# A list scheduler's rates: measured TensorE times, a delay for a change of grid, and one port for VectorE and GpSimd

## The chip, the cores and the metric

The kernel runs on one core of a Trainium2 chip. The metric is the device time of the whole program in microseconds (us), the median of several runs. A core has five engines that matter here: TensorE (PE in the profile; its weight loads are PEld), VectorE (DVE), ScalarE (ACT), GpSimd (POOL) and SyncE (SP), which issues the transfers. Each engine executes its own queue strictly in order and waits on semaphores for the others. SBUF is the on-chip memory; PSUM holds the products of TensorE.

## What is computed

The reference is a decoder trunk of two layers for one sequence of 512 tokens and 1024 channels in float32. Each layer has three sub-layers, each with a norm before it and a residual sum behind it:

```python
for l in range(DEPTH):                                   # DEPTH = 2
    h = rms_norm(x, norm_mix[l])
    p_a, p_b, p_c, p_d = jnp.split(h @ w_in[l], splits, axis=-1)
    y = jnp.concatenate([
        rglru_group(p_a, ...),        # a gated linear recurrence
        retention_group(p_b, ...),    # chunked decay attention, 4 heads
        rwkv7_group(p_c, ...),        # RWKV-7, 4 heads
        ssd_group(p_d, ...)],         # Mamba-2 SSD, 4 heads
        axis=-1)
    x = x + y @ w_out[l]
    x = x + memory_cross_attention(rms_norm(x, norm_mem_q[l]), rms_norm(mem, norm_mem_kv[l]), ...)
    x = x + swiglu(rms_norm(x, norm_ffn[l]), ffn_w_in[l], ffn_w_out[l])
return rms_norm(x, norm_final)
```

## The kernel before

**Recording and ordering.** The trunk is written as straight-line code (class `Trunk`), but its calls issue nothing. Each call is recorded as an `Op` with its tiles and its predecessors (`Sched.record`), and `Sched.cost` gives it a duration `dur` and a latency `lat` in nanoseconds, worked out from its shapes. `Sched.order` then makes one static order for all engines. It keeps a clock for each engine. In each step it looks, for each engine, at all operations whose predecessors are placed, and takes the one with the smallest key: the earliest possible start, then the class `cls`, then the largest `rank` (the longest chain of durations behind the operation). `Sched.place` lets an operation start only when a buffer of its tile's kind is free. `Sched.issue` (L511, so that line stands on every row of the profile) emits the operations in that order. The model's times decide the order and nothing else; on the chip each engine runs its part of the order in order.

**Tiles.** The kinds that matter are `s` (a 128x512 float32 tile in SBUF, 70 of them), `u`, `v`, `w` (a block of weights as loaded, its upper part and its lower part, three buffers each), `a` (PSUM banks for the dense products, 3), `b` (PSUM banks for all the rest, 5), `t` (small statistics), `q` (the state in RWKV's loop), `n` (32-row tiles, 2). A name such as `s_1012_1620` is the kind, the number of the recorded operation that first writes it, and a running number.

**Dense products.** A float32 product is made as three float32r products of two-part operands. `weights` loads a block into `u` (SP), casts the upper part `v` (ACT) and subtracts for the lower part `w` (DVE, or POOL for some gate projections, which `project` does late). For 128 output columns `project` issues 24 matmuls 128x512 over one `a` bank: eight blocks of the contraction times (v with the upper part of x, v with its lower part, w with the upper part). The dense products form the chain "d": they keep their recorded order. All other TensorE work (`b` banks, float32, shapes from 128x1 to 128x512) is side work, which the scheduler puts between them.

**The mixers.** `mix` projects w_in and runs the four groups beside each other. `rwkv_pair` (two heads each, so two pairs a layer) first inverts a triangular matrix by a substitution of 62 steps on POOL on tiles `n`, copies the result, sends it out and back in another layout (`fd<-n`, `s<-fd`), and then runs a loop of eight chunks, in which TensorE, DVE and ACT hand one small state (`q`) to each other. `ssd` and `retention` work in four chunks or blocks and end with a norm, `head_norm` and `rsqrt`, in which DVE issues some ten small operations 128x8 one after the other (a Newton iteration). The mixers' results are the input of `w_out`. Then follow `cross` and `ffn`, which are almost wholly dense, and at the end `finish`.

**What orders the work around the change**: `cost` (durations, from which both the model's starts and the ranks come) and `order` (the key, the clocks of the engines).

## Time and profile before

| | |
|---|---|
| median of the runs | 1730.94 us (1729.71 to 1733.04, three runs) |
| span of the profiled execution | 1729.7 us |
| TensorE busy | 1675.9 us, 97% |
| VectorE, ScalarE, GpSimd busy | 1039.6, 632.2, 329.1 us |
| chain of work that ended last | PE 83%, DVE 9%, ACT 2% |

The profile is of one execution. The span counts from its first instruction to its last. TensorE's busy time is modelled at the instructions' ends, so it is read together with the starts of successive matmuls. The granted clock (PEclk) stands as a share of the full 2.4 GHz; 0.50 is the lower level of 1.2 GHz, and a value between is a mean over a stretch that had both.

### The profile page before, as it was taken

To read this page: it belongs to the slowest core of one execution; us is meant where nothing else is said; L and a number is where in the kernel's file an instruction comes from. 1 tells how busy PE (TensorE), PEld (TensorE's weight loads), DVE (VectorE), ACT (ScalarE), POOL (GpSimd) and SP (SyncE) were. 2 spreads that over 40 slices of the span, in tenths; PEclk is the share of its full clock that TensorE was granted. 3 is DMA by queue.
4 is the path that set the end of the run, shared out by engine and by line. 5 is a ranking of instruction groups with operands and counts; after the bars stand their busy time and mean duration, and the time that the engine had idled before them with its cause. 6 is when DMAs were issued, how large, how long until landed. Compare 5 with 4: busy or idle time off the path is not lost.

```text
span 1729.7 us, 21681 instructions
## 1 busy us (share of the span) xinstructions
PE 1675.9 (97%) x8344; PEld 1355.9 (78%) x8344; DVE 1039.6 (60%) x1712; ACT 632.2 (37%) x976; POOL 329.1 (19%) x370
## 2 busy tenths in 40 slices
PE   7999999999999999999989999989999999999997
PEld 6687777888788888888878877767887888888886
DVE  7777669775664555432467767596665655544323
ACT  6434244543542233322344333354444423332221
POOL 3367724300000000000141875241000000000001
PEclk9899999999999999999999999999999999999998
DMA  7433321441333333333453333115322333333331
GB/s 231 129 83 101 87 55 37 152 128 50 98 97 98 95 89 97 95 101 119 137 153 88 88 89 90 37 37 173 95 74 86 98 97 89 94 98 91 93 95 63
DMA packets 296648, 168.99 MB, mean 98 GB/s; under 512 B 19424, under 2 KB 283872, under 8 KB 296416
## 3 DMA queue, kind: packets, MB, share of 16 engines
q1 hardware_dynamic: 296544, 167.60, 33.4%
q8 instruction: 66, 1.08, 0.3%
q14 instruction: 38, 0.31, 0.1%
HBM read 156.04 MB, written 9.44 MB: 96 GB/s over the span
## 4 chain that ended last, share of the span: by engine, by line
PE 83%; DVE 9%; ACT 2%; issue 1%; DMA 1%; POOL 1%; SPq 0%; DVEq 0%; ACTq 0%; POOLq 0%
PE a L511 73%; PE b L511 9%; DVE s L511 5%; DVE t L511 2%; DVE w L511 1%; ACT s L511 1%; ACT v L511 1%; DMA s<-s 1%; DVE q L511 0%; POOL s L511 0%; DMA s<-in_lora_dram 0%; POOL n L511 0%; SPq L511 0%; DMA n<-nd 0%; ACT L511 0%
## 5 line engine op out<-in xcount | busy, mean ns | idle before, releaser
L511 PE MATMUL a<-s,v 128*128 128x512 f32 (+1 forms) x4012 | 1252.7, 391 | 15.9 <-ACT s L511 9.3
L511 PEld LDWEIGHTS a<-s,v 128*128 128x128 f32 x4012 | 748.0, 191 | 177.6 <-DVE s L511 10.9
L511 PE MATMUL a<-s,w 128*128 128x512 f32 (+1 forms) x2006 | 782.8, 390 | 3.8 <-DVE w L511 1.9
L511 ACT CAST v<-u 128x1024 fp32r<-128x1024 f32 (+3 forms) x275 | 282.0, 1026 | 673.2 <-PE a L511 390.2
L511 PEld LDWEIGHTS a<-s,w 128*128 128x128 f32 x2006 | 382.8, 191 | 83.7 <-POOL w L511 2.3
L511 DVE TENSOR_TENSOR w<-u,v 128x1024 fp32r<-128x1024 f32 (+3 forms) x242 | 294.7, 1219 | 148.3 <-ACT v L511 145.3
L511 DVE TENSOR_TENSOR s<-a,s 128x512 f32<-128x512 f32 (+1 forms) x132 | 90.7, 691 | 259.5 <-PE a L511 240.4
L511 POOL TENSOR_TENSOR w<-u,v 128x1024 fp32r<-128x1024 f32 x33 | 81.9, 2483 | 657.3 <-ACT v L511 646.0
L511 ACT ACTIVATE s<-s 128x512 f32<-128x512 f32 (+3 forms) x229 | 142.8, 628 | 128.6 <-DVE s L511 111.9
L511 POOL TENSOR_TENSOR s<-s,s 128x512 f32<-128x512 f32 (+3 forms) x45 | 57.1, 1286 | 589.2 <-ACT s L511 555.9
L511 PEld LDWEIGHTS b<-s,s 128*128 128x128 f32 (+3 forms) x1268 | 127.2, 165 | 43.7 <-issue 15.3
L511 PE MATMUL b<-s,s 128*128 128x128 f32 (+8 forms) x1268 | 154.6, 269 | 5.5 <-DVE s L511 4.0
L511 DVE TENSOR_TENSOR s<-s,s 128x512 f32<-128x512 f32 (+3 forms) x184 | 133.0, 726 | 26.4 <-ACT s L511 18.5
L511 DVE SCALAR_TENSOR_TENSOR s<-s,s 128x512 f32<-128x512 f32 (+2 forms) x164 | 122.8, 752 | 13.3 <-ACT s L511 12.7
L511 DVE TENSOR_TENSOR s<-s,a 128x512 f32<-128x512 f32 (+1 forms) x49 | 33.2, 678 | 102.0 <-PE a L511 102.0
L511 POOL TENSOR_TENSOR s<-n,n 32x31 f32<-32x31 f32 (+15 forms) x124 | 73.4, 592 | 97.4 <-DMA n<-nd 88.0
L511 POOL TENSOR_TENSOR n<-n,s 32x31 f32<-32x31 f32 (+15 forms) x124 | 81.6, 658 | 9.7
L511 ACT COPY s<-b 64x128 f32<-64x128 f32 (+3 forms) x108 | 35.0, 325 | 113.9 <-PE b L511 93.3
L511 PE MATMUL a<-v,s 128*128 128x260 f32 (+1 forms) x256 | 68.3, 344 | 0.0
L511 DVE SCALAR_TENSOR_TENSOR s<-s,prm,s 128x512 fp32r<-128x512 f32 (+3 forms) x78 | 63.0, 832 | 7.4 <-ACT s L511 7.3
L511 PE MATMUL b<-cst,s 128*128 128x128 f32 (+2 forms) x312 | 47.6, 266 | 10.7 <-DVE s L511 8.4
L511 PEld LDWEIGHTS b<-cst,s 128*128 128x128 f32 x312 | 38.6, 159 | 20.5 <-issue 8.0
(93 smaller groups left out, 835.0 us busy)
## 6 DMA issues: line engine op xcount, KB each, us to landing
u<-in_ffn_w_in_dram SPq DMA_DIRECT2D x88, 512.0 KB
u<-in_w_in_dram SPq DMA_DIRECT2D x52, 512.0 KB
u<-in_ffn_w_out_dram SPq DMA_DIRECT2D x32, 512.0 KB
u<-in_mem_wv_dram SPq DMA_DIRECT2D x16, 512.0 KB
u<-in_w_out_dram SPq DMA_DIRECT2D x16, 512.0 KB
u<-in_mem_wq_dram SPq DMA_DIRECT2D x16, 512.0 KB
u<-in_mem_wo_dram SPq DMA_DIRECT2D x16, 512.0 KB
u<-in_mem_wk_dram SPq DMA_DIRECT2D x13, 512.0 KB
```

What stands on the lines that cost most here:

```text
L511: op.fn(*[real(x) for x in op.args], **{k: real(x) for k, x in op.kw.items()})
```

## The change

Comments and docstrings go; they produce nothing. What stays differs in two methods. In `cost`, the durations of TensorE's operations are new: a transpose 85 ns for 112; a float32r product `max(111, 6 + 0.4405 w)`, which makes a 128x512 product 231.5 ns for 217; a float32 product, which used to be proportional to its size, has a floor, 116 ns where the stationary operand has at most 64 columns and 219 ns above it. A scan on DVE costs twice as much, a copy on POOL about half. Each TensorE operation gets a `grid` (64 or 128 rows by 64 or 128 columns). Operations of DVE with two wide operands in SBUF, some single-operand ones from SBUF to SBUF, and all POOL operations get the flag `port`. In `order`, an operation with that flag starts in the model only when the other engine's last flagged operation has ended; among TensorE operations of equal start and class, one with the grid of the last one goes first, ahead of the rank; and a change of grid advances the model's time by 93 ns.

```diff
             if fn == "transpose":
-                op.dur = 112.0
+                op.dur = 85.0
             else:
-                m, w = _free(ins[0]), _free(ins[1])
-                op.dur = (max(2 * m, w) / 2.4 if ins[0].ap.dtype == F32R else max(m, w) * 1.667) + 4
+                k, m, w = ins[0].shape[0], _free(ins[0]), _free(ins[1])
+                op.grid = HD if k <= HD else P, HD if m <= HD else P
+                if ins[0].ap.dtype == F32R:
+                    op.dur = max(111.0, 6 + 0.4405 * w)
+                else:
+                    op.dur = 2 * max(58.0 if m <= HD else 109.5, 2.5 + w / 1.2)
...
+            elif fn == "tensor_tensor_scan":
+                rate = 2.08
...
-            rate = {"tensor_tensor": 2.3, "tensor_copy": 3.5, "memset": 0.83}.get(fn, 1.2)
+            rate = {"tensor_tensor": 2.3, "tensor_copy": 1.9, "memset": 0.83}.get(fn, 1.2)
...
+        if op.eng in ("DVE", "POOL") and not op.bytes:
+            wide = [x for x in ins if isinstance(x, Ref) and x.root.kind not in "ab" and _free(x) > 1]
+            op.port = len(wide) > 1 or op.eng == "POOL" or (
+                fn in ("tensor_scalar", "tensor_copy") and len(wide) == 1 and not in_psum and out.root.kind not in "ab")
...
+                    if op.port:
+                        t = max(t, held[other[e]])
...
-                    key = (t, op.cls if op.cls != 2 or side < 1500.0 else 0, -op.rank, op.n)
+                    key = (t, op.cls if op.cls != 2 or side < 1500.0 else 0, op.grid != grid if e == "PE" else False, -op.rank, op.n)
...
+            if e == "PE" and op.grid != grid:
+                grid = op.grid
+                t += 93.0
...
+            if op.port:
+                held[e] = end
```

No instruction is added, dropped or reshaped, and no tile or buffer count changes. The line that issues moves from L511 to L535. What changes is the order on every engine. Three places in the first layer show it.

The first place is GpSimd in the second pair's substitution (`n_1010`, steps of two operations each; `w<-u,v` is the lower part of a block of weights for a late projection). Before:

```order
L511 TENSOR_TENSOR s_1012_1620<-n_1006_1513,n_1010_1601 32x112
L511 TENSOR_TENSOR n_1010_1601<-n_1010_1601,s_1012_1620 32x4x28
L511 TENSOR_TENSOR w_2128_2076<-u_2126_1807,v_2127_2057 128x1024
L511 TENSOR_TENSOR s_1012_1620<-n_1006_1513,n_1010_1601 32x87
L511 TENSOR_TENSOR n_1010_1601<-n_1010_1601,s_1012_1620 32x3x29
L511 TENSOR_TENSOR s_1012_1620<-n_1006_1513,n_1010_1601 32x60
L511 TENSOR_TENSOR n_1010_1601<-n_1010_1601,s_1012_1620 32x2x30
```

After:

```order
L535 TENSOR_TENSOR w_2291_2331<-u_2289_2071,v_2290_2307 128x1024
L535 TENSOR_TENSOR s_1012_1664<-n_1006_1606,n_1010_1584 32x112
L535 TENSOR_TENSOR n_1010_1584<-n_1010_1584,s_1012_1664 32x4x28
L535 TENSOR_TENSOR s_1748_1574<-s_1748_1574,t_1971_2311 128x512
L535 TENSOR_TENSOR w_2321_2378<-u_2319_2169,v_2320_2367 128x1024
L535 TENSOR_TENSOR s_1012_1664<-n_1006_1606,n_1010_1584 32x87
L535 TENSOR_TENSOR s_2060_2157<-s_2060_2157,s_2061_2119 128x512
L535 TENSOR_TENSOR n_1010_1584<-n_1010_1584,s_1012_1664 32x3x29
L535 TENSOR_TENSOR w_2354_2443<-u_2352_2252,v_2353_2423 128x1024
L535 TENSOR_TENSOR s_1012_1664<-n_1006_1606,n_1010_1584 32x60
```

One `w` and no full-width tile stood between the substitution's last 20 steps; now eight `w` and six full-width tiles do.

The second place is TensorE in the loop of the second pair, where `ssd`'s products (`b_1654`, `b_1672`, `b_1685`) stand beside it; `a` are dense products. Before:

```order
L511 MATMUL b_1210_2566<-s_1110_2217,s_1004_1231 64x64
L511 MATMUL b_1654_2561<-s_1635_1965,s_1648_2017 64x128 x3
L511 MATMUL b_1672_2612<-cst,t_1399_1554 128x128
L511 MATMUL b_1685_2614<-cst,s_1432_1391 128x128
L511 MATMUL b_1672_2612<-cst,t_1399_1554 128x128
L511 MATMUL b_1685_2614<-cst,s_1498_1488 128x128
L511 MATMUL a_2201_2486<-s_118_592,v_2199_2237 128x512
L511 MATMUL b_1672_2612<-cst,t_1399_1554 128x128
```

After:

```order
L535 MATMUL b_1654_2788<-s_1635_2722,s_1648_2764 64x128
L535 MATMUL b_1175_2812<-s_1105_2575,s_1097_1266 128x128
L535 MATMUL a_2391_2569<-v_2431_2600,s_23_197 128x512
L535 MATMUL a_2391_2569<-w_2432_2617,s_23_197 128x512
L535 MATMUL a_2391_2569<-v_2431_2600,s_24_211 128x512
L535 MATMUL b_1672_2836<-cst,t_1399_1713 128x128 x3
L535 MATMUL b_1685_2841<-cst,s_1432_1372 128x128
L535 MATMUL b_1685_2841<-cst,s_1498_1472 128x128
```

Side products of one kind stand together, and so do dense ones.

The third place is TensorE at the end of the mixers: the transposes that close retention's norm (`b_2007`, `b_2012`), ssd's (`b_2249`, `b_2254`) and the second pair's (`b_1264`). Before (`b_1264` has been issued 20 rows earlier, `a_2322` is a projection of w_in):

```order
L511 MATMUL a_2322_2948<-s_117_537,w_2321_2694 128x512
L511 MATMUL b_2007_2877<-cst,s_1749_1690 128x128 x2
L511 MATMUL b_2012_2883<-cst,s_1749_1690 128x128 x2
L511 MATMUL a_2322_2948<-s_120_521,v_2320_2665 128x512
L511 MATMUL b_2249_3006<-cst,t_2239_2964 128x128 x4
L511 MATMUL b_2254_3012<-cst,t_2239_2964 128x128 x4
L511 MATMUL a_2322_2948<-s_121_558,v_2320_2665 128x512
```

After (`a_2469` is the first product of w_out, begun before the last four chunks of the loop):

```order
L535 MATMUL b_1236_3044<-s_1110_2608,s_1004_1229 64x64
L535 MATMUL b_2007_3091<-cst,s_1748_1574 128x128 x2
L535 MATMUL b_2012_3100<-cst,s_1748_1574 128x128 x2
L535 MATMUL b_2249_3153<-cst,t_2239_3093 128x128 x4
L535 MATMUL b_2254_3160<-cst,t_2239_3093 128x128 x2
L535 MATMUL b_1264_3163<-cst,s_945_978 128x128 x4
L535 MATMUL b_2254_3160<-cst,t_2239_3093 128x128 x2
L535 MATMUL a_2469_2888<-s_2453_3175,v_2467_2733 128x512
```

All three norms' transposes now stand together behind the loop's last product, with no dense product between them; before, projections of w_in stood between and behind them.

## Rows read from the trace of the kernel before

**Rows 1.** The page: busy time of each engine, and the chain that ended last.

```profile
PE 1675.9 (97%) x8344; PEld 1355.9 (78%) x8344; DVE 1039.6 (60%) x1712; ACT 632.2 (37%) x976; POOL 329.1 (19%) x370
PE 83%; DVE 9%; ACT 2%; issue 1%; DMA 1%; POOL 1%; SPq 0%; DVEq 0%; ACTq 0%; POOLq 0%
```

**Rows 2.** Windows by stage: start:end, length, busy (instructions) by engine, clock, DMA.

```profile
0.00:100.00 100.00, 84.55 (x452) 70.20 (x453) 77.39 (x158) 50.85 (x84) 28.80 (x24) 0.91 0.55 165
100.00:350.00 250.00, 242.27 (x1417) 191.39 (x1417) 185.44 (x373) 101.04 (x175) 132.85 (x162) 0.99 0.32 88
...
850.00:900.00 50.00, 44.42 (x277) 40.48 (x276) 28.91 (x29) 18.89 (x29) 28.33 (x14) 0.93 0.48 138
900.00:1200.00 300.00, 286.10 (x1614) 222.69 (x1613) 217.41 (x434) 120.26 (x204) 134.15 (x165) 0.98 0.31 85
1200.00:1700.00 500.00, 499.55 (x2216) 406.09 (x2216) 256.57 (x331) 167.38 (x236) 0.00 (x0) 1.00 0.32 92
```

**Rows 3.** Windows of 50 us around the ends of the mixers, same columns.

```profile
250.00:300.00 50.00, 46.67 (x283) 36.64 (x283) 46.71 (x126) 23.71 (x43) 21.95 (x17) 0.97 0.14 43
...
1100.00:1150.00 50.00, 46.89 (x288) 36.43 (x287) 45.07 (x112) 25.31 (x46) 20.21 (x16) 0.97 0.10 33
1150.00:1200.00 50.00, 44.62 (x186) 34.56 (x185) 37.91 (x66) 22.85 (x34) 13.89 (x8) 0.93 0.43 132
```

**Rows 4.** Timeline of PE in pair two's loop: start, us, instruction, count, [idle before].

```profile
231.63 0.50 PE L511 MATMUL a<-s,v 128*128 128x512 f32 x1
231.97 0.40 PE L511 MATMUL a<-s,w 128*128 128x512 f32 x1
232.20 0.38 PE L511 MATMUL b<-s,s 128*128 128x128 f32 x2
...
234.03 0.48 PE L511 MATMUL a<-s,v 128*128 128x512 f32 x1
234.44 0.44 PE L511 MATMUL b<-q,s 64*64 64x64 f32 x4
```

**Rows 5.** Timeline of PE: two chunks' first products of the loop; transposes after a wait.

```profile
244.73 0.38 PE L511 MATMUL b<-q,s 128*128 128x128 f32 x2
...
250.11 0.39 PE L511 MATMUL b<-q,s 128*128 128x128 f32 x2
...
293.69 1.79 PE L511 MATMUL b<-cst,s 128*128 128x128 f32 x15 [2.08 <-DVE s L511]
```

**Rows 6.** DVE from 100 to 350 us by form: count | busy, mean ns | idle before.

```profile
L511 DVE SCALAR_TENSOR_TENSOR t<-t,t 128x8 f32<-128x8 f32 x31 | 6.6, 217 | 0.5
...
L511 DVE TENSOR_REDUCE t<-s 128x8 f32<-128x512 f32 x8 | 5.5, 682 | 2.6 <-ACT s L511 2.4
L511 DVE TENSOR_SCALAR t<-t 128x8 f32<-128x8 f32 x8 | 5.2, 654 | 0.1
...
L511 DVE SCALAR_TENSOR_TENSOR q<-b,t,cst 128x128 f32<-128x128 f32 x14 | 4.9, 348 | 10.0 <-PE b L511 10.0
...
L511 DVE TENSOR_TENSOR t<-t 128x8 f32<-128x8 f32 x15 | 4.6, 310 | 0.2
...
L511 DVE SCALAR_TENSOR_TENSOR s<-s,prm,b 128x512 f32<-128x512 f32 x3 | 2.2, 745 | 1.2 <-PE b L511 1.2
```

**Rows 7.** Timeline of DVE: a small operation of the Newton iteration, twice.

```profile
27.45 2.29 DVE L511 SCALAR_TENSOR_TENSOR t<-t,t 128x4 f32<-128x4 f32 x1
...
297.19 0.17 DVE L511 SCALAR_TENSOR_TENSOR t<-t,t 128x8 f32<-128x8 f32 x1
```

**Rows 8.** Timeline of POOL: weight blocks at 27 us and in pair two's substitution.

```profile
27.35 2.36 POOL L511 TENSOR_TENSOR w<-u,v 128x1024 fp32r<-128x1024 f32 x1 [0.96 <-ACT v L511]
...
202.32 2.37 POOL L511 TENSOR_TENSOR w<-u,v 128x1024 fp32r<-128x1024 f32 x1 [6.49 <-ACT v L511]
```

**Rows 9.** Timeline of SP's issues: the transfers behind pair two's substitution.

```profile
207.18 2.39 SPq L511 DMA_DIRECT2D fd<-n  x2
...
215.21 3.93 SPq L511 DMA_DIRECT2D s<-fd  x8
```

More of the change, by code (lines that the diff above doesn't have):

```diff
@@ L233 @@
     __slots__ = ("n", "eng", "fn", "args", "kw", "dur", "lat", "preds", "succ", "left", "ready", "end", "rank", "cls",
-                 "roots", "first", "chain", "bytes", "start", "table")
+                 "roots", "first", "chain", "bytes", "start", "table", "grid", "port")
 def _free(x):
@@ L364, in cost @@
         op.bytes = 0
-        op.table = None
+        op.table = op.grid = None
+        op.port = False
         op.lat = 170.0
@@ L373, in cost @@
             op.lat = 200.0
+            op.grid = P, P
             if fn == "transpose":
-                op.dur = 112.0
+                op.dur = 85.0
             else:
-                m, w = _free(ins[0]), _free(ins[1])
-                op.dur = (max(2 * m, w) / 2.4 if ins[0].ap.dtype == F32R else max(m, w) * 1.667) + 4
+                k, m, w = ins[0].shape[0], _free(ins[0]), _free(ins[1])
[4 more added lines that the diff above has]
+                    op.dur = 2 * max(58.0 if m <= HD else 109.5, 2.5 + w / 1.2)
         elif op.eng == "ACT":
@@ L426, in order @@
         table = None
+        grid = P, P
+        held = {"DVE": 0.0, "POOL": 0.0}
+        other = {"DVE": "POOL", "POOL": "DVE"}
         INF = float("inf")
```

## The prediction

> **What bounds the kernel now.** The page first: TensorE is busy 1675.9 of 1729.7 us and carries 83% of the chain that ended last, VectorE another 9% [rows 1]. No instruction changes, so the kernel can gain only what TensorE waits, what it loses at a lower clock, and what it pays for the order of its own products. The windows by stage say where that is [rows 2]. In cross attention and FFN TensorE works 499.55 of 500 us at clock 1.00: nothing to gain, and dense products in a fixed order leave the scheduler little to spoil. What is idle lies in the head (0 to 100: 15.5 us, clock 0.91), in the two mixers (100 to 350: 250 - 242.27 = 7.7 us; 900 to 1200: 300 - 286.10 = 13.9 us) and between the layers (850 to 900: 5.6 us, clock 0.93). The windows of 50 us place the mixers' share at their ends and give the clock: 0.97, 0.97 and 0.93 over 46.67, 46.89 and 44.62 busy us cost 0.03 x 46.67 = 1.4, 0.03 x 46.89 = 1.4 and 0.07 x 44.62 = 3.1 us [rows 3]. So both mixers together now lose 7.7 + 1.4 + 13.9 + 4.5 = **27.5 us**. That is the number to beat.
>
> **Part 1: fewer changes between kinds of products.** In the loop, a dense product behind another starts the next one 0.23 us later (231.97 to 232.20); the first one behind side work takes 0.34 (231.63 to 231.97); one with side work of another grid on both sides 0.41 (234.03 to 234.44) [rows 4]. So a return costs 0.11 and a departure to another grid 0.07 to 0.1; I take 0.1 for each. Counted in the two orders, grid changes fall from 317 to 288 (29 fewer) and returns to a dense product behind another grid from 124 to 112 (12 fewer): 41 x 0.1 = 4.1 us. Returns behind side work of the same grid fall from 156 to 121; each costs between 0 (no row shows one bare) and the 0.11 above, so 0 to 3.9 us, of which I take 1.6, nearer the lower end because a change of grid is what the dear rows have in common. Part 1: **-5.7 us** (-4.1 to -8.0). It lies on TensorE, which is the bound, so nothing hides it except a wait for another engine right behind.
>
> **Part 2: the ends of the mixers.** Here the order does something the diff does not say. On GpSimd the second pair's substitution now shares the queue with eight weight blocks and six full-width operations. A block takes 2.37 us [rows 8], and it cannot start before TensorE frees one of three buffers, which happens once a projection: 24 x 0.23 = 5.5 us. So the substitution ends later, and the pair's loop, counted in TensorE work since the start, moves from about 194 to 241 us (second layer: 1029 to 1069), while gate projections and the recurrent group come earlier. Before the last four chunks only six dense products are left, and behind the loop none (third place of the order). Three terms for each layer:
>
> *The tail.* Behind the last chunk DVE has to issue, before w_out can go on, 32 small operations, two reduces, two multiplications with statistics, two operations with a PSUM bank and seven more of full width. With the rows: the reduces 2 x 0.68; the eleven of full width at 0.7, an estimate between the reduce's 0.68 and the 0.745 of an operation with a PSUM bank (7.7), or all at 0.745 (8.2); the small ones at 0.17 where nothing is in the way [rows 7] or at the mean of what they took in this stage, (31 x 0.217 + 15 x 0.310 + 8 x 0.654) / 54 = 0.305 [rows 6]. That is 1.4 + 7.7 + 5.4 = 14.5 or 1.4 + 8.2 + 9.8 = 19.4 us. TensorE's own work meanwhile is 20 transposes at 1.79 / 15 = 0.12 [rows 5] and some thirty small products at the 0.11 of [rows 4], together about 6. It waits 8.5 to 13.4 us; I take 10.6, a little under the middle, since GpSimd has three operations there against the weight blocks of before.
>
> *The loop.* A chunk's chain is nowhere bare. It is at most 5.4 us (244.73 to 250.11, with dense products in it [rows 5]) and at least some 3.2: three DVE steps of some 0.35 [rows 6], an ACT copy that I put at the same, and four visits of TensorE of 0.4 to 0.5 [rows 4, 5]. I take the middle, 4.3. The last four chunks have 3 to 4 us of other TensorE work each, say 3.5: 4 x 0.8 = 3.2 us of waiting (0 to 7.6).
>
> *The clock.* A stretch of this much idle time cost 1.4 to 3.1 us at the lower level behind it [rows 3]; 2.3.
>
> Sum for a layer 10.6 + 3.2 + 2.3 = 16.1, both 32.2. Two waits on the first pair's data, at about 109 and 953 us, stand at the same products in both orders; I leave 2 us for them. So the mixers lose 34.2 after and 27.5 before: **+6.7 us**.
>
> **Part 3: head and change of layer.** In the new order all eight products of the memory's keys come before the first norm's results are used; before, the norm stood in the middle of them. DVE's small operations for that norm still stand behind weight blocks. The products no longer wait for them, the norm's users do, and there is no other work for TensorE behind. Of 15.5 and 5.6 idle us [rows 2] the early part is loading and stays. I take 0 for each, with 3 us to both sides: one block of 2.36 us in or out of DVE's way, with its clock [rows 8].
>
> **Part 4: DVE and GpSimd kept apart.** That the two hinder each other is plain: a small operation that takes 0.17 us took 2.29 while GpSimd's block ran from 27.35 for 2.36 us [rows 7, 8]. But the plan keeps them apart only in its own time, and the queues have no wait for it; it is worth what the new order happens to avoid. Its share is inside the 0.17 and 0.305 of part 2 and the 3 us of part 3. The planner flags every GpSimd operation, pure fills too, so it plans some avoidable delays, none of which is a wait on the chip. The Trainium skill, page "SBUF — State Buffer", section "Who interferes with whom", says that the shared port goes to one engine for a whole instruction and the other fully blocks, and that a DVE instruction with two SBUF inputs contends only with a GpSimd instruction that reads SBUF, not with one that only writes. The rows agree with the first half; no row shows the second. By that rule each of the tail's three GpSimd operations, half as wide as the 2.37 us block and so some 1.2 us each, blocks DVE for up to 3.6 us in a layer, and the tail goes from 14.5 to 18.1; if the port were shared, it would stay at 14.5. Both are inside the range above.
>
> **The sum.** -5.7 + 6.7 + 0 = +1.0 on the profiled span of 1729.7, which gives 1730.7. The median is 1.2 above that span, so the time is **1732 us**.
>
> **Rivals.** *Keeping apart pays (faster).* If the new order really spares DVE its collisions, the small operations run at 0.17 wherever TensorE waits for them. The tails come to 8.5 us each, the loop to 2, the clock to 1.4: 12 a layer, 24 + 2 - 27.5 = -1.5. Head and change of layer give 3 each for the same reason: -1.5 - 6 - 5.7 = -13, which is **1718 us**. For it: the small operations in this stage lost 54 x (0.305 - 0.17) = 7.3 us [rows 6, 7]. Against it: most of that was beside dense work and cost nothing, and the new tail has no dense work.
>
> *GpSimd's queue holds up the second loop (slower).* From the freeing of the last block's buffer to the loop TensorE has some 16.4 us of work in the new order. The chain that must fit is the block, 2.4 us [rows 8], with its cast ahead of it, put at half of that, the last step of 0.3, and the way out and back, from the first issue to the end of the last 215.21 + 3.93 - 207.18 = 12.0 [rows 9], with a landing behind it that no row bounds and that is left at 0 to 2: 16 to 18 us. It decides when that exceeds 16.4. Then the loop starts 0 to 2 us late, its chunks run at the 5.4 of before (7.6 us of waiting instead of 3.2), and the tail stands at its upper end: 2 + 7.6 + 13.4 + 3.1 = 26 a layer at worst, 24.5 in the middle; 49 + 2 - 27.5 - 5.7 = +18, which is **1749 us**. For it: no dense product is left to fill in, so every us of delay is lost. Against it: the late start alone is worth 2 us, and the rest takes the upper value of each term.
>
> *The change does little that it says.* Only part 1 is real and the ends of the mixers lose what they lost: 1725 us. It is the lower edge of my forecast.
>
> **How the numbers follow.** My forecast, 1732, with its own range 1724 to 1740, has 0.42; faster through separation, 1712 to 1726, has 0.29; the late loop, 1738 to 1755, has 0.29. A measurement tells about 0.2%, or 3.5 us, from no change. Of the forecast's 0.42, 0.25 lies within that, 0.08 below and 0.09 above. So faster 0.08 + 0.29 = 0.37, the same 0.25, slower 0.09 + 0.29 = 0.38. The range 1714 to 1750 leaves out about 0.08 below and 0.1 above.
>
> **What would show it.** Right: cross attention and FFN unchanged; 100 to 350 and 900 to 1200 us each lose about 16 us in idle time and clock, now in one block before w_out, released by DVE's small operations; fewer starts of 0.34 between dense products. Rival one: TensorE's wait before w_out is under 9 us and the head under 13 idle. Rival two: GpSimd's blocks in the substitution wait for buffers, TensorE waits before the loop's first product, and its chunks stand 5 us apart. Wrong altogether: waits in places that the order leaves as they were, or another time for cross attention or FFN.

## The result and the profile after

The changed kernel is slower: **1741.3 us** (four runs, 1740.9 to 1742.5) against 1731.6 us for the kernel before beside it, a ratio of **1.006 with an interval of 1.0046 to 1.0074**. The profiled executions differ by the same: spans of 1739.6 and 1729.7 us. Medians, ranges and intervals, here and below, leave out two executions that ran slow, one of the kernel without the port rule (1781.5 us) and one with TensorE's times alone (2056.3 us). The forecast had been 1732 and no change. 1741 lies inside the whole range (1714 to 1750) and on the side to which the prediction gave 0.38, but above the forecast's own 1724 to 1740 and among the times of the late-loop rival, 1738 to 1755.

Where the 9.9 us are is best read at one product that both traces hold. The dense products keep their order, so the start of one and the same matmul can be compared:

| the same dense product, about | before, us | after, us | later by | added in this stage |
|---|---|---|---|---|
| first w_in products behind the head | 101.9 | 100.5 | -1.4 | -1.4 |
| within w_out, first layer | 335.7 | 346.3 | +10.6 | **+12.0** (mixers) |
| end of FFN, first layer | 850.3 | 860.9 | +10.6 | 0.0 |
| first w_in products, second layer | 933.4 | 941.1 | +7.7 | -2.9 (change of layer) |
| behind w_out, second layer | 1220.7 | 1230.1 | +9.4 | **+1.7** (mixers) |
| end of FFN, second layer | 1717.7 | 1725.7 | +8.1 | -1.3 |

The rest, 1.8 us, is in the last 14 us. Nearly all of the loss is made in the two mixers. The page agrees: TensorE is no longer busy for 97% of the span, as in [rows 1].

```profile
PE 1673.1 (96%) x8344; PEld 1358.0 (78%) x8344; DVE 1025.0 (59%) x1712; ACT 634.9 (36%) x976; POOL 317.3 (18%) x370
```

The windows of the changed kernel, cut at those products and at the ends of the mixers, say how. Columns as in [rows 2]: window, length, busy us of PE, PEld, DVE, ACT and POOL, clock, DMA share, GB/s.

```profile
100.50:291.50 191.00, 184.95 (x1081) 146.00 (x1080) 136.34 (x240) 73.44 (x123) 118.74 (x148) 1.00 0.32 85
300.00:333.00 33.00, 22.01 (x162) 17.68 (x162) 25.76 (x89) 11.11 (x25) 6.50 (x8) 0.84 0.09 24
333.00:346.30 13.30, 13.07 (x51) 10.59 (x51) 7.02 (x10) 4.67 (x7) 0.00 (x0) 0.87 0.19 59
941.10:1150.00 208.90, 202.53 (x1175) 160.42 (x1174) 149.72 (x275) 81.61 (x136) 123.33 (x157) 1.00 0.33 88
1150.00:1186.00 36.00, 24.91 (x180) 19.82 (x178) 28.65 (x94) 12.99 (x30) 6.49 (x8) 0.86 0.08 23
1186.00:1200.00 14.00, 13.76 (x54) 11.06 (x54) 7.53 (x11) 4.70 (x7) 0.00 (x0) 0.88 0.18 57
```

And the same cut through the kernel before:

```profile
101.90:285.00 183.10, 178.22 (x1124) 139.11 (x1122) 132.50 (x284) 69.86 (x129) 110.74 (x148) 1.00 0.29 75
285.00:335.70 50.70, 47.85 (x224) 39.15 (x225) 41.78 (x73) 24.00 (x35) 20.45 (x12) 0.97 0.32 99
933.40:1137.00 203.60, 197.47 (x1203) 154.25 (x1202) 143.08 (x299) 74.22 (x136) 111.62 (x150) 1.00 0.29 76
1137.00:1192.90 55.90, 48.52 (x214) 37.20 (x213) 45.22 (x80) 24.36 (x36) 22.54 (x16) 0.91 0.31 91
```

Idle time plus clock, as in the prediction, gives this table (the 0.3 us from 291.5 to 300 go with the first line):

| | before | after |
|---|---|---|
| first layer, up to the last chunks | 4.9 | 6.3 |
| first layer, from there into w_out | 2.85 + 0.03 x 47.85 = 4.3 | 11.2 + 0.16 x 22.0 + 0.13 x 13.07 = 16.4 |
| second layer, up to the last chunks | 6.1 | 6.4 |
| second layer, from there into w_out | 7.4 + 0.09 x 48.52 = 11.8 | 11.3 + 0.14 x 24.9 + 0.12 x 13.76 = 16.5 |
| both mixers | **27.1** | **45.6** |

So by these windows the two ends lose 16.4 and 16.5 us. The clock's share in that is too large: the stretches at the lower level lie largely in the waits, and the mean of a long window charges them to the busy time. Summed over windows of 5 us, the clock costs 3.6 and 3.8 us in the changed mixers, the ends lose 14.9 and 15.1, and both mixers together 42.7 for 27.3 before.

The timeline of TensorE in the changed kernel shows the bare end. Columns: start, us, instruction and count, in brackets the idle time before it and its releaser.

```profile
316.95 0.44 PE L535 MATMUL b<-q,s 64*64 64x64 f32 x4
317.32 1.95 PE L535 MATMUL b<-cst,s 128*128 128x1 f32 x16
319.20 0.65 PE L535 MATMUL b<-s,s 128*64 128x64 f32 x4
319.78 1.12 PE L535 MATMUL b<-cst,s 128*128 128x128 f32 x4
326.61 1.11 PE L535 MATMUL b<-cst,s 128*128 128x128 f32 x4 [5.71 <-POOL s L535]
...
331.26 0.49 PE L535 MATMUL a<-s,v 128*128 128x512 f32 x1 [1.29 <-ACT s L535]
```

Retention's norm is closed by two groups of four transposes, one for each of its result tiles (the third place of the order shows the first group alone). From the first group, at 319.78, to the second, at 326.61, TensorE's queue holds nothing else. The releaser named is GpSimd, but it is only the last link: VectorE's chain of small operations ahead of it runs from 319.3 with one pause of 0.15 us. One piece of it:

```profile
324.99 0.16 DVE L535 SCALAR_TENSOR_TENSOR t<-t,t 128x8 f32<-128x8 f32 x1
...
325.20 1.37 DVE L535 SCALAR_TENSOR_TENSOR t<-t,t 128x8 f32<-128x8 f32 x3
```

```profile
325.51 1.04 POOL L535 TENSOR_TENSOR s<-s,t 128x512 f32<-128x512 f32 x1 [5.73 <-DVE t L535]
328.19 2.67 POOL L535 TENSOR_TENSOR s<-s,s 128x512 f32<-128x512 f32 x2 [1.64 <-ACT s L535]
```

Three small operations at 325.20 take 1.37 us together where 0.17 is the time of one: GpSimd's operation starts at 325.51, and they are done when it is. The Trainium skill, page "SBUF — State Buffer", section "Who interferes with whom", says that the other engine fully blocks; this trace agrees, with one collision of some 1 us at a layer's end, not the three (3.6 us) that the prediction held possible.

The clock falls around the wait. From 320 to 325 us, with TensorE busy for 0.89 us of 5, it is at 0.50. It was not the long wait that took it down: that begins at 320.9, and the window before, with TensorE busy for 4.73 of 5, is already at 0.93. What came ahead is the loop's last chunks, in which TensorE waited for 3.67 us of 17. Every window up to 340 holds some of the lower level:

```profile
300.00:317.00 17.00, 13.33 (x115) 10.61 (x115) 12.60 (x39) 4.11 (x12) 1.74 (x4) 1.00 0.16 44
315.00:320.00 5.00, 4.73 (x41) 4.33 (x39) 3.23 (x11) 1.78 (x5) 1.04 (x1) 0.93 0.02 3
320.00:325.00 5.00, 0.89 (x4) 0.49 (x3) 4.71 (x29) 1.33 (x3) 0.00 (x0) 0.50 0.01 2
325.00:330.00 5.00, 3.36 (x16) 3.11 (x16) 3.97 (x14) 2.05 (x4) 2.86 (x3) 0.55 0.00 2
330.00:335.00 5.00, 3.19 (x8) 2.13 (x9) 4.99 (x8) 2.87 (x6) 0.86 (x1) 0.79 0.00 0
335.00:340.00 5.00, 5.00 (x20) 4.00 (x20) 1.65 (x3) 2.03 (x3) 0.00 (x0) 0.87 0.00 0
```

Why are the ends bare? GpSimd's timeline says it. The copy behind the second pair's substitution starts at 258.49 in the changed kernel; it used to start at 207.22, with the first of [rows 9]. It stands behind the eight blocks of weights, seven of them with a wait of 1.6 to 3 us for ScalarE's cast, which mostly waits for TensorE:

```profile
248.34 2.50 POOL L535 TENSOR_TENSOR w<-u,v 128x1024 fp32r<-128x1024 f32 x1 [2.00 <-ACT v L535]
250.79 0.28 POOL L535 TENSOR_TENSOR s<-n,n 32x60 f32<-32x60 f32 x1
...
254.61 2.40 POOL L535 TENSOR_TENSOR w<-u,v 128x1024 fp32r<-128x1024 f32 x1 [1.58 <-ACT v L535]
...
258.49 2.10 POOL L535 COPY n<-n 32x1024 f32<-32x1024 f32 x1
```

So the loop of the second pair begins at 278.6 us for 227.4 before, and the projections that used to lie beside its last chunks have been used up by then.

### The profile page after: what moved, and what is told of

Read it like the earlier page. It is cut to its first block, busy times and chain, and to the rows that moved or that the text cites. A ratio compares the mean times of both kernels' runs of the same rounds, so it can differ in the third digit from the quotient of the medians.

```text
span 1739.6 us, 21636 instructions
## 1 busy us (share of the span) xinstructions
PE 1673.1 (96%) x8344; PEld 1358.0 (78%) x8344; DVE 1025.0 (59%) x1712; ACT 634.9 (36%) x976; POOL 317.3 (18%) x370
## 5 line engine op out<-in xcount | busy, mean ns | idle before, releaser
L535 PE MATMUL a<-s,v 128*128 128x512 f32 (+1 forms) x4012 | 1240.3, 389 | 18.9 <-ACT s L535 11.4
L535 PEld LDWEIGHTS a<-s,v 128*128 128x128 f32 x4012 | 745.8, 190 | 182.7 <-DVE s L535 13.0
L535 PE MATMUL a<-s,w 128*128 128x512 f32 (+1 forms) x2006 | 778.6, 388 | 0.3 <-DVE w L535 0.3
L535 ACT CAST v<-u 128x1024 fp32r<-128x1024 f32 (+3 forms) x275 | 282.4, 1027 | 717.3 <-PE a L535 438.5
L535 PEld LDWEIGHTS a<-s,w 128*128 128x128 f32 x2006 | 380.6, 190 | 80.8 <-issue 0.7
L535 DVE TENSOR_TENSOR w<-u,v 128x1024 fp32r<-128x1024 f32 (+3 forms) x242 | 290.7, 1202 | 166.1 <-ACT v L535 164.1
L535 DVE TENSOR_TENSOR s<-a,s 128x512 f32<-128x512 f32 (+1 forms) x132 | 90.6, 690 | 264.7 <-PE a L535 246.9
L535 POOL TENSOR_TENSOR w<-u,v 128x1024 fp32r<-128x1024 f32 x33 | 79.1, 2398 | 622.3 <-ACT v L535 621.7
L535 ACT ACTIVATE s<-s 128x512 f32<-128x512 f32 (+3 forms) x229 | 142.7, 628 | 128.2 <-DVE s L535 104.9
L535 POOL TENSOR_TENSOR s<-s,s 128x512 f32<-128x512 f32 (+3 forms) x45 | 50.5, 1138 | 642.8 <-ACT s L535 566.1
L535 PE MATMUL b<-s,s 128*64 128x64 f32 (+8 forms) x1268 | 152.8, 269 | 12.8 <-DVE s L535 8.1
L535 PEld LDWEIGHTS b<-s,s 128*128 128x128 f32 (+3 forms) x1268 | 124.7, 164 | 46.8 <-issue 15.9
L535 DVE TENSOR_TENSOR s<-s,s 128x512 f32<-128x512 f32 (+3 forms) x184 | 131.0, 717 | 18.8 <-ACT s L535 12.2
L535 DVE SCALAR_TENSOR_TENSOR s<-s,s 128x512 f32<-128x512 f32 (+2 forms) x164 | 116.1, 712 | 8.8 <-ACT s L535 7.8
L535 DVE TENSOR_TENSOR s<-s,a 128x512 f32<-128x512 f32 (+1 forms) x49 | 33.2, 677 | 104.4 <-PE a L535 104.4
L535 POOL TENSOR_TENSOR s<-n,n 32x31 f32<-32x31 f32 (+15 forms) x124 | 73.3, 591 | 97.2 <-DMA n<-nd 82.9
L535 POOL TENSOR_TENSOR n<-n,s 32x31 f32<-32x31 f32 (+15 forms) x124 | 82.4, 664 | 8.8
L535 PE MATMUL a<-v,s 128*128 128x260 f32 (+1 forms) x256 | 71.5, 353 | 2.6 <-DVE s L535 2.6
L535 ACT COPY s<-b 64x128 f32<-64x128 f32 (+3 forms) x108 | 34.8, 324 | 89.4 <-PE b L535 70.5
L535 DVE SCALAR_TENSOR_TENSOR s<-s,prm,s 128x512 fp32r<-128x512 f32 (+3 forms) x78 | 57.4, 759 | 11.0 <-ACT s L535 11.0
L535 PE MATMUL b<-cst,s 128*128 128x128 f32 (+2 forms) x312 | 50.4, 277 | 14.1 <-POOL s L535 11.4
L535 PEld LDWEIGHTS b<-cst,s 128*128 128x128 f32 x312 | 40.5, 164 | 22.9 <-POOL s L535 12.2
```

What stands on the lines that cost most here:

```text
L535: op.fn(*[real(x) for x in op.args], **{k: real(x) for k, x in op.kw.items()})
```

## The experiments

Two theories went in. **P**: the port rule in the plan makes the second substitution late and the ends bare. **G**: the grid rule, which bunches side products, does. In what follows every time is a median beside the kernel before on the same chip, with the ratio's interval.

**Without the port rule.**

```diff
-                    if op.port:
-                        t = max(t, held[other[e]])
```

> The changed kernel without the two lines by which a flagged operation waits for the other engine in the plan; TensorE's new times, the grid rule and the two new rates stay. Theory P (the port rule in the plan empties the ends of the mixers: it makes GpSimd's second substitution late, weight blocks slip in, and the dense products are used up before the last chunks): the two bare tails of some 16 us a layer go, since in this order 139 and 119 dense products stand among the last 100 side products of the mixers where the changed kernel has none; the tails lose at most what they lost before, so the time is 1722 to 1730 us. Rival G (the grid rule, which bunches side products, makes the ends bare): it is still in, so the time stays at 1737 to 1742 us.

Measured: 1766.9 us (1755.0 to 1769.9), 1.0182 (1.0127 to 1.0236). Both theories missed. The ends are covered, as P said, but another loss appears in the middle. With nothing held back, side work is drawn forward, VectorE is busy for 9.80 of 10 us, TensorE waits 2.65 us in ten, and then the clock falls:

```profile
215.00:225.00 10.00, 7.35 (x69) 5.08 (x70) 9.80 (x25) 3.03 (x7) 1.35 (x3) 1.00 0.31 80
225.00:270.00 45.00, 44.60 (x175) 34.95 (x175) 19.60 (x56) 6.18 (x16) 5.51 (x4) 0.51 0.05 12
270.00:285.00 15.00, 14.42 (x79) 10.10 (x78) 12.38 (x29) 6.36 (x13) 4.70 (x3) 1.00 0.10 25
```

It stays at its lower level for 45 us in which TensorE is busy for 44.6: 0.49 x 44.6 = 22 us, more than the whole difference in question. TensorE issues side products with a dense one now and then in that stretch. Summed over windows of 5 us, this kernel is idle for 10 us more than the kernel before and loses 27 us more to the clock. What follows: in this order the port rule also does good. That the wait of 2.65 us is what took the clock down is argued, not shown; if it is, a wait can cost many times its own length.

**The port rule alone, in the kernel before.** The same lines and flags are put into the kernel before, with its old TensorE times and without the grid rule.

> The kernel before with the port rule alone (old TensorE times, no grid rule, old rates). Theory P: the same late substitution, with nine weight blocks in it and 15 and 17 dense products among the last 100 side products; bare tails, some 10 us a layer more than before: 1738 to 1752 us. Rival G: as before, 1729 to 1734 us.

Measured: 1779.8 us (1777.0 to 1783.7), 1.0275 (1.0247 to 1.0303). P's direction, but far beyond its price, and the place is in part another one. The ends lose (310 to 360 us: 8.5 idle, clock 0.73), and TensorE also waits in the middle of both mixers, for VectorE, once for 8.1 us in the first and once for 11.7 in the second. The row has the total, the number of waits and the longest:

```profile
PE a L522 <- DVE s L522: 31.6, 15, 11.7
```

That the rule, with TensorE's work underrated in the plan, delays side work so far that dense products wait for it is an explanation that no run isolates.

**The grid rule alone** (with the two new rates of VectorE and GpSimd; no port rule, old TensorE times).

```diff
-                op.dur = 85.0
+                op.dur = 112.0
...
-                    if op.port:
-                        t = max(t, held[other[e]])
```

> The changed kernel without the port rule and with the old TensorE times: what is left is the grid rule with its 93 ns and the two rates. 296 changes of grid for 317 before and 539 alternations of dense and side products for 585, dense products at the ends as in the kernel before (130 and 105 among the last 100). Theory P: 3 to 6 us under the kernel before, 1725 to 1729 us. Rival G: bare ends, 1738 to 1742 us.

Measured: 1734.7 us (ten runs, 1729.2 to 1741.5), 1.0022 (1.0002 to 1.0042). G falls for the grid rule by itself: the ends are not bare. P's gain of 3 to 6 us does not come either. From 205 to 285 us TensorE is idle for 8.1 us (1.1 in the kernel before), more than the 3 to 6 us that fewer changes of grid were to give.

```profile
205.00:285.00 80.00, 71.87 (x446) 55.91 (x447) 65.88 (x169) 31.58 (x59) 21.86 (x17) 0.96 0.13 37
```

**Without the preference for the last grid.**

```diff
-                    key = (t, op.cls if op.cls != 2 or side < 1500.0 else 0, op.grid != grid if e == "PE" else False, -op.rank, op.n)
+                    key = (t, op.cls if op.cls != 2 or side < 1500.0 else 0, -op.rank, op.n)
```

> The changed kernel without the preference for the last grid in the key; port rule, 93 ns and times stay. Four weight blocks in the second substitution for eight, 100 dense products among the last 100 side products in both layers, and 312 grid changes. If bare ends are what costs, whichever rule makes them: the tails go, some 12 us in all, and part 1's gain goes with them: 1728 to 1735 us. If the port rule costs by something other than the bare ends (DVE delayed by the plan all over): 1738 to 1745 us.

Measured: 1735.4 us (1733.2 to 1739.1), 1.0020 (1.0009 to 1.0031); 6 us under the changed kernel, 0.4 above what bare ends as the cause allow. The ends still lose, 7.8 and 7.9 us idle with clocks of 0.85 and 0.89 (300 to 345 and 1150 to 1195 us): with four weight blocks in the substitution for eight, the pair's loop starts at 246 us for 279. So beside the port rule the grid rule has a share after all: its preference doubles the blocks.

**Late weights on VectorE, in the changed kernel.** Theory **T** from here on: the bare ends are what the change costs, and they come from the late substitution. Rivals: **V**, VectorE's load makes the ends long; **C**, the clock decides, wherever a wait takes it down.

```diff
-        late = lambda c0: self.project(w, c0, hat, self.G)
+        late = lambda c0: self.project(w, c0, hat)
```

> The changed kernel with one word gone: the late gate projections take the lower parts of their weights on VectorE instead of GpSimd (33 blocks). No weight block stands in GpSimd's second substitution any more (eight before), 83 dense products stand among the last 100 side products of the mixers in both layers (none in the changed kernel), 36 among the last 40. Theory T (the bare tails, which come from the late substitution, are what the change costs): each layer's loss from the last chunks to w_out falls from some 16 us to 5 to 8; VectorE's 33 x 1.2 = 40 us more are beside dense work; 1720 to 1731 us. Rival V (VectorE is what the tails wait for, so more work on it keeps them long): 1738 to 1750 us. Rival C (a wait that takes the clock to its lower level decides, wherever it lies): a stretch of 20 us or more at 0.50, 1750 us or more.

Measured: 1728.6 us (1725.8 to 1735.0), 0.9987 (0.9974 to 1.0000): 12.7 under the changed kernel, as T said; V falls. The trace puts it where T has it: of 13.0 us in the span, 12.8 are in the mixers, and 11.1 of these are idle time at the ends, 11.2 and 11.3 us before the edit and 5.7 each after it. But the copy behind the substitution still starts at 225.3, and with the clock the ends lose more than the 5 to 8 us a layer that T allowed. (The edit moves 14 blocks, not the 33 of the expectation: VectorE's go from 216 to 230. The other 19 are the values' weights, four a layer, and those of the head and the change of layer.)

**The same in the kernel before, as a control.**

> The same word gone in the kernel before, as a control: 85 and 107 dense products among the last 100 side products for 75 and 97, so the ends stay covered. Theory T: nothing to cure, 1727 to 1735 us, so what the edit gives the changed kernel comes from its tails. Rival V: VectorE's added 40 us lengthen the ends here too, 1738 us or more.

Measured: 1710.1 us (1709.5 to 1712.7), 0.9878 (0.9863 to 0.9893). The control gains more than the case, 21 us where no end was bare, so the time of the first is no proof by itself; what speaks for T there is the place. TensorE is idle for 10.5 us less and loses 10 us less to the clock. What changed beside the order is that GpSimd's blocks of 2.5 us meet fewer of VectorE's small operations. Counted in the trace of the kernel before, 97 of the 142 operations 128x8 ran beside no GpSimd operation at all, and none of these took over 0.173 us; the seven that ran beside a weight block took 1.9 us on average. In this kernel two do. Two of their forms, over the whole run, in the kernel before and in this one:

```profile
L511 DVE SCALAR_TENSOR_TENSOR t<-t,t 128x8 f32<-128x8 f32 x84 | 22.6, 275 | 1.4
L511 DVE TENSOR_SCALAR t<-t 128x8 f32<-128x8 f32 x16 | 9.8, 610 | 0.2
```

```profile
L511 DVE SCALAR_TENSOR_TENSOR t<-t,t 128x8 f32<-128x8 f32 x84 | 16.9, 207 | 1.4
L511 DVE TENSOR_SCALAR t<-t 128x8 f32<-128x8 f32 x16 | 4.0, 250 | 0.1
```

275 to 207 ns and 610 to 250 ns for the same instructions. That collisions lengthen these operations is shown; that this is the reason for the 21 us is argued: the edit reorders everything else, too.

**GpSimd free in the plan.** This one takes half of the rule away and leaves the blocks where they are. In `order`, an engine with an equal start wins if it stands earlier in the list, and VectorE stands ahead of GpSimd. As the code reads, with both engines waiting for each other VectorE's next flagged operation and GpSimd's become possible at the same instant, and VectorE takes it each time; GpSimd's steps wait for a gap.

```diff
-                    if op.port:
+                    if op.port and e == "DVE":
                         t = max(t, held[other[e]])
```

> The changed kernel with the port rule for VectorE alone: in the plan GpSimd no longer waits for VectorE, which takes every tie and so starves it; VectorE still waits for GpSimd. The second substitution holds no weight block, 151 and 131 dense products among the last 100 side products. Theory T: tails covered, 1720 to 1731 us. Rival C: as in the kernel without the port rule, side work is drawn forward, VectorE falls behind around 210 us, and TensorE's waits there take the clock to 0.50 for tens of us: 1750 to 1775 us.

Measured: 1720.8 us (1715.1 to 1723.6), 0.9932 (0.9913 to 0.9952), **20.5 us under the changed kernel** by four words. T holds. The copy behind the substitution starts at 197.47 for 258.49, and both ends are covered without a gap and at full clock (38.20 of 38.20 us, 60.00 of 60.00):

```profile
197.47 2.02 POOL L535 COPY n<-n 32x1024 f32<-32x1024 f32 x1
```

```profile
105.00:300.00 195.00, 190.19 (x1174) 149.06 (x1173) 141.24 (x316) 75.60 (x138) 115.43 (x158) 0.97 0.26 69
300.00:338.20 38.20, 38.20 (x171) 31.10 (x170) 28.20 (x36) 19.21 (x26) 14.35 (x7) 1.00 0.47 141
931.70:1140.00 208.30, 200.84 (x1225) 159.22 (x1224) 157.07 (x349) 79.99 (x145) 115.97 (x157) 0.97 0.27 70
1140.00:1200.00 60.00, 60.00 (x265) 48.79 (x264) 42.24 (x49) 27.80 (x40) 17.93 (x9) 1.00 0.50 155
```

The ends' loss (32.9 us by the long windows, 30 by the short ones) is gone. Some 11 come back as idle time and clock in the middle (4.8 + 0.03 x 190 and 7.5 + 0.03 x 201, together 24 for 12.7 in the changed kernel), and the head takes 105.0 us for 100.5. The half of the rule that makes VectorE wait stayed in, and a fall of the clock for 45 us as in the first experiment did not happen.

**Both edits.**

> Both edits: GpSimd does not wait in the plan, and the late weights' lower parts are VectorE's. 78 and 108 dense products among the last 100 side products. Theory T: 1718 to 1730 us. Rival C: if the clock falls behind waits in the middle of the mixers as in the kernel without the port rule, 1750 us or more; if the dense products left for the ends are what keeps the clock up there, under 1735.

Measured: 1715.2 us (1713.1 to 1718.7), 0.9906 (0.9891 to 0.9921), 2.8 us under T's range and far from C's 1750.

Set side by side, the kernels with a trace show T's first half as a scale. The idle time is TensorE's in the first layer, in the 46.3 us up to the product that starts at 346.3 us in the changed kernel:

| kernel | copy behind the substitution, us | idle at the end, us |
|---|---|---|
| changed | 258.5 | 11.2 |
| port rule alone | 257.0 | 7.5 |
| without the preference for the last grid | 228.7 | 7.9 |
| late weights on VectorE | 225.3 | 5.7 |
| before | 207.2 | 2.7 |
| GpSimd free; both edits | 197.5; 198.7 | 0.0; 0.0 |
| control; without the port rule; grid rule alone | 196.0; 191.5; 189.8 | 1.3; 1.5; 2.0 |

The total times do not follow this scale, because the same edits also make or remove waits elsewhere.

**The tail itself, shortened in a fixed order.** All edits above make a new order. These two keep the order of the changed kernel, and of the kernel before, instruction for instruction, and leave 54 small operations of VectorE out.

```diff
+        cut = {n + 5488 * l for l in range(2) for a in (1254, 1997, 2240) for n in range(a, a + 9)}
...
-                op.fn(*[real(x) for x in op.args], **{k: real(x) for k, x in op.kw.items()})
+                if op.n not in cut:
+                    op.fn(*[real(x) for x in op.args], **{k: real(x) for k, x in op.kw.items()})
```

> The changed kernel, its order on every engine as it is, with 54 instructions of VectorE not issued: the nine refining steps of the root in the second norm of retention, in ssd's and in the second pair's norm, in both layers (so these norms keep the first guess of the root). They take 0.13 to 0.2 us each, one in the first layer 1.0, so some 4.5 us a layer. Theory T (with no dense product beside it, VectorE's chain at the mixers' ends is paid in full): nearly all of it comes back, 3 to 4.5 us a layer and some clock, 1731 to 1735 us, 6 to 10 under the changed kernel. Rival M (the tail waits for something else, a transfer, GpSimd or ScalarE, and the small operations lie beside it): under 3 us, 1738 to 1742 us.

Measured: 1742.6 us (eleven runs, 1734.9 to 1747.7), 1.0052 (1.0037 to 1.0068). By the median, nothing came back, as M said. The profile caught the shortest of the runs (1734.9 us, span 1733.1), and in that run T is right about the waits: the one for GpSimd is 3.36 us for 5.71, and the ends' idle time falls from 11.0 to 33 - 24.72 = 8.3 and from 11.1 to 36 - 28.00 = 8.0.

```profile
323.48 1.11 PE L538 MATMUL b<-cst,s 128*128 128x128 f32 x4 [3.36 <-POOL s L538]
```

```profile
300.00:333.00 33.00, 24.72 (x166) 19.75 (x165) 23.56 (x64) 11.40 (x25) 6.33 (x8) 0.79 0.07 19
1150.00:1186.00 36.00, 28.00 (x181) 22.44 (x181) 24.58 (x66) 12.36 (x26) 6.31 (x8) 0.81 0.07 20
```

The clock is lower in these windows, 0.79 and 0.81 for 0.84 and 0.86, but between the same products as in the first table the mixers take 2.6 and 2.9 us less, so little of the 5.8 us less idle time is lost to it in this run. The other ten runs are 4 to 13 us longer. Their mean granted clock is 0.977 to 0.983, in the profiled run 0.983; no trace of them shows where they lose.

> The same 54 instructions not issued in the kernel before, its order as it is: there they lie beside projections of w_in, and TensorE waits behind them for 2.1 and 0.6 us in the first layer, 1.2, 1.7 and 0.6 in the second. Theory T: hidden but for a part of these waits, 1 to 4 us, 1727 to 1730 us. If the small operations cost the same here as in the changed kernel (6 to 10 us), it is not the missing dense products that expose them.

Measured: 1723.8 us (1722.8 to 1726.3), 0.9943 (0.9924 to 0.9962): 7.8 us, more than T allowed. At the same products as in the first table, the two mixers give 2.0 and 2.1 of it, T's upper figure. Of the rest, 3.9 us lie between products where nothing was left out and no order differs, 2.4 in the head and 1.5 in the change of layer, and nearly all of that is clock: 0.95 and 0.97 where [rows 2] have 0.91 and 0.93, by the mean of these windows 0.04 x 84.6 + 0.04 x 44.2 = 5.2 us.

```profile
0.00:100.00 100.00, 84.65 (x466) 70.29 (x466) 78.20 (x160) 52.70 (x87) 31.66 (x28) 0.95 0.57 170
850.00:900.00 50.00, 44.22 (x281) 39.77 (x279) 31.49 (x32) 21.21 (x33) 26.69 (x14) 0.97 0.53 150
```

So this pair did not settle what it was made for: 5.5 us in the mixers of the profiled run with bare ends, 4.1 with covered ones. It shows that waits at the ends follow VectorE's chain, and that a few us of idle time are no measure of the time as long as the clock may move by as much.

**TensorE's times alone, in the kernel before.**

> The kernel before with TensorE's new durations alone. No weight block in the second substitution, 92 and 81 dense products among the last 100 side products, 325 grid changes for 317. Theory T: the ends stay covered, so 1727 to 1735 us, and the true times bring little by themselves. Rival C (side work drawn forward makes waits in the middle of the mixers that take the clock down, as in the kernel without the port rule, which has these times): 1745 us or more.

Measured: 1748.5 us (1740.0 to 1762.3), 1.0092 (1.0058 to 1.0126). T's range is missed, and the time lies in C's. The only trace is that of the execution left out, so where the kernel loses, and whether by C's cause, stays open.

**A mixture of rules by stage.** The late weights on VectorE, the old rules for everything up to the second layer's first norm, and from there on the changed rules with GpSimd free: every new branch of `cost` is under `op.n >= 5540`.

> A mixture of what was best by stage: late weights' lower parts on VectorE in both layers, the kernel before's rules for the first layer, and from the second layer's first norm on the changed rules with GpSimd not waiting in the plan. From the two kernels it is made of, landmark to landmark: head 99.3 and first mixers 228.5 us as with the old rules, change of layer 79.2 and second mixers 273.1 as with the new ones, for 81.5 and 275.5: some 4.7 us under the old rules with the late weights moved (1710), 1703 to 1709 us. If stages don't carry over (the rest of the order shifts what they wait for), 1709 us or more.

Measured: **1705.0 us** (1704.8 to 1709.9), 0.9838 (0.9816 to 0.9861), inside the 1703 to 1709 worked out from the stages. By stage the working is less exact: the head took 103.1 us for 99.3 with the very same order, the second mixers 270.5 for 273.1. It is the fastest kernel here, 1.6% under the kernel before and 2.1% under the changed one. TensorE is busy for 98% of the span, and the second layer's end has no gap.

```profile
PE 1661.9 (98%) x8344; PEld 1350.9 (79%) x8344; DVE 1027.3 (60%) x1726; ACT 632.9 (37%) x976; POOL 293.1 (17%) x356
```

```profile
1100.00:1196.00 96.00, 96.00 (x448) 77.77 (x447) 68.19 (x125) 45.30 (x68) 20.76 (x11) 1.00 0.43 132
```

## Why the prediction was right, and where it was not

**What bounds the kernel**: right. Cross attention and FFN are unchanged (0.0 us in the first layer, 1.3 less with all that follows in the second). The loss before, 27.5 us in the mixers, is 27.1 by windows cut at the products.

**Part 1, grids**: the direction and the prices were right; how much of it reaches the time stays open. Counted over the mixers of both traces, on dense products of full width that follow one another without a wait and at full clock: 0.23 us to the next product between two dense ones; 0.34 behind side work of another grid (96 such before, 86 after); 0.33 ahead of it (48 and 31); 0.43 with both (11 and 6); and 0.31 behind side work of the same grid, where the prediction stayed nearer to nothing. What they cost over 0.231 us falls from 23.0 to 16.3, so 6.7 us for a forecast of 5.7 (4.1 to 8.0). By the stages less is left: the mixers' idle time and clock rose by 45.6 - 27.1 = 18.5 us, the mixers by 12.0 + 1.7 = 13.7, and the 4.8 between is what TensorE saved on all its products; with the clock summed over windows of 5 us it is 42.7 - 27.3 - 13.7 = 1.7. Where the difference went stays open.

**Part 2, the ends**: the mechanism and the size were right. 16.1 us a layer forecast, 14.9 to 16.5 measured, by either way to count the clock. Its pieces were less so, and their misses partly cancel. In the first layer the loop's waits are 3.67 for 3.2, the tail is 7.5 for 10.6 and under its own 8.5 to 13.4, and the clock 3.6 (5.2 by the long windows) for 2.3. (The mean of the small operations, 0.305 in the prediction, is 0.308 by its own terms, which changes no sum.) The late loop is where the order said it would be, and the half of the port rule that causes it is shown by the kernel with GpSimd free.

**The step that failed** is the sentence after that: "Two waits on the first pair's data ... I leave 2 us for them." Up to the last chunks the changed kernel waits 6.3 and 6.4 us, 12.7 for 2. The two waits that were named are indeed the only ones that stand at the same product in both orders, and they came to 1.23 + 1.18 = 2.4 us. What was put at nothing is that the new order makes waits of its own. Matched product by product, and counting waits over 0.15 us, 8.3 us of the old waits ahead of the last chunks are gone, as the sum assumed, and 9.8 us of new ones stand at other products. Some of the largest, first in the kernel before, then in the changed kernel; the first line of each is the wait that stayed:

```profile
109.39 1.16 PE L511 MATMUL b<-s,s 64*128 64x128 f32 x8 [1.13 <-DVE s L511]
204.99 0.46 PE L511 MATMUL b<-q,s 128*128 128x128 f32 x2 [1.52 <-DVE q L511]
1064.97 0.63 PE L511 MATMUL b<-cst,s 128*128 128x128 f32 x4 [2.10 <-DVE s L511]
```

```profile
108.33 1.13 PE L535 MATMUL b<-s,s 64*128 64x128 f32 x8 [1.23 <-DVE s L535]
163.55 0.99 PE L535 MATMUL b<-s,s 64*64 64x64 f32 x26 [1.00 <-DMA s<-fd]
266.78 0.50 PE L535 MATMUL a<-v,s 128*128 128x512 f32 x1 [1.32 <-DVE s L535]
1119.89 0.50 PE L535 MATMUL a<-v,s 128*128 128x512 f32 x1 [1.29 <-DVE s L535]
```

Had the sum allowed as much for new waits as the old order lost there, 4.9 + 6.1 = 11.0, it would have been 32.2 + 11.0 - 27.5 - 5.7 = +10.0, 1741 us; the result is 1741.3. That this comes out so close is largely luck: they are not the same waits, part 1 left 1.7 to 4.8 us for 5.7, and head (-1.4), change of layer (-2.9) and last stage also enter.

**Part 3**: right within its 3 us to each side (-1.4 and -2.9). **Part 4**: right in that the plan's separation is no wait on the chip; VectorE's small operations did become shorter (219 ns for 275 on the commonest form), but at the ends they now stood alone. **Rival one** came in part: the small operations ran faster and the tails waited under 9 us, but the head stayed at 14.5 us idle, and the waits in the middle were new. **Rival two** has the time (1738 to 1755) and two of its three signs: GpSimd's blocks wait for buffers, and from 294.19 to 314.33 us the last chunks stand 4.1 to 5.8 us apart, 5.0 on average. Its prices did not come: TensorE does not wait for the loop to begin, the chunks cost 3.67 us of waiting and not 7.6, and the tail did not reach its upper end.

## What to carry to other kernels

When a change moves work in a plan, sum the waits of the old trace by place, and do not put the new order's at nothing because they can't be named: here 8.3 us of old waits went and 9.8 us of new ones came elsewhere. Where a planner lets two engines exclude each other, see which of them it makes wait: here four words that let GpSimd go took 20 us off (that the tie in particular is the fault was read from the code; no run changes the tie alone). And look at what is left to run beside the last dependent chain; here the plan had used up the dense products before it.

## What the hardware showed that was not expected

The granted clock can stay at its lower level through a stretch in which TensorE is almost never idle: 45 us with 44.6 busy, at 0.51, while side products filled the queue and dense products came singly. The same loop in the kernel before, 229 to 272 us, ran at 1.00 with 64 dense products for 21, and the changed kernel's 300 to 317 us ran at 1.00 with no dense product and 3.67 us of waiting. So what holds the clock down there stays open. The wait ahead of it was 2.65 us in ten; if that began it, a small wait cost 22. And head and change of layer moved by 3.9 us, nearly all of it clock, in a kernel whose order there was the same as before. Both make differences under some 0.3% hard to put down to a cause in this kernel.
